# Local attention's mask: from a TensorE product to a VectorE addition in PSUM, with the score products of two heads written in turn

## The chip, the core and the metric

The kernel runs on one core of a Trainium2 chip. The metric is the device time of one execution in microseconds (us); the median of the runs counts.

## What is computed

A two-layer backbone over 256 context tokens and 256 latent tokens, width 1024. Each layer mixes tokens by three branches (a state space branch "S5", a latent attention "MLA", a windowed local attention), merges them by gates and an output projection, and then runs a mixture of 16 experts. The last layer updates the latent tokens alone. The part that matters here is the local attention of 8 query heads over 2 key heads, width 64:

```python
def window_branch(qc, kc, vc, ql, kl, vl, sink, row, col, update_ctx):
    ...
    valid = (jnp.abs(j - BLOCK - r) <= WINDOW) & (key_pos >= 0) & (key_pos < L)
    s_band = jnp.einsum('bnqkgd,bnskd->bnkgqs', qb, kb).astype(jnp.float32) * WIN_SCALE
    s_band = jnp.where(valid[None, :, None, None], s_band, NEG_INF)
    s_ctx = jnp.einsum('bnqkgd,bskd->bnkgqs', qpb, kc).astype(jnp.float32) * WIN_SCALE
    sk = jnp.broadcast_to(sink.astype(jnp.float32)[None, None, :, :, None, None], s_ctx.shape[:-1] + (1,))
    p = jax.nn.softmax(jnp.concatenate([s_band, s_ctx, sk], axis=-1), axis=-1)
    ...
    out_c = None
    if update_ctx:
        ...
        out_c = dense_attention(q_c, kc, vc, WIN_SCALE, sink).reshape(B, Lc, WIN_Q_HEADS * WIN_HEAD_DIM)
```

With 256 latent tokens and blocks of 128 there are two blocks of queries, and each sees the keys of both; the mask cuts one triangle of the block that is not its own.

## The kernel before

Everything is float32. A product that needs the full precision is made of three TensorE products of operands split into a high and a low part (`mm3`, line 411). A head is 64 wide, so the operands of one head lie on 64 partitions, rows 0 to 63 for the even head of a pair and rows 64 to 127 for the odd one.

`win_branch` (line 1237) runs once in each layer. It goes over 4 pairs of heads `hp` and 2 blocks of queries `qt`. For each it takes two PSUM tiles named `sc` (there are two such buffers in all, line 187), one for each head `a`, and fills each with 512 scores: three products for the context keys (columns 0 to 255), three for the latent keys (256 to 511), and one product of the identity with a constant mask of 128 x 128 that is accumulated onto 128 of these columns (line 1261). That product is in full float32 and appears as two records in the trace. `softmax` (line 1014) then reads the tile: VectorE takes the maximum of a row (`tensor_reduce`, line 1024), joins the sink (1025 to 1028), ScalarE takes the exponential (line 1031), VectorE sums, inverts and scales (1034 to 1037). After both blocks `attend` transposes the probabilities on TensorE into tiles `tp` and multiplies them with the values into `mm`. In the first layer (`full`) there are also two context tiles for each pair, with six products each and no mask.

TensorE's gaps are filled: `tick` issues work of other parts, in the first layer branch projections (tiles `F`) and products for the modulation parameters of later groups (tiles `ad`); in the second layer branch projections alone. The program goes through a scheduler that orders each engine's instructions ahead of the run; each engine then goes through its own list strictly in order. Weights come by DMAs that the SP queue issues.

After the local attention come the latent attention, the output projection and the layer norm, then the experts, whose 192 tiles of weights of 1 MB stream through a ring of buffers.

Of the kernel before, what the change touches and what calls it, by code (L numbers as in the profile page):

```python
# [31 lines left out]
# ---------------------------------------------------------------- shape-only constants  # L32
# [68 lines left out]
# ---------------------------------------------------------------- memory map of SBUF  # L101
class Arena:
    """column ranges of one SBUF tile; the range that has been free for longest is given first"""
# [31 lines left out]
    def alloc_at(self, name, at, want):  # L135
        """the columns at .. at + want, which are free"""
        assert name not in self.live and at % self.G == 0, name
        at, need = at // self.G, (want + self.G - 1) // self.G
        assert at + need <= self.n and None not in self.stamp[at:at + need], (name, self.live)
        return self.take(name, at, want)  # L140
# [17 lines left out]
class Net:  # L158
# [6 lines left out]
    # ------------------------------------------------------------ helpers  # L165
# [6 lines left out]
    def rot(self, name, cols, n, low=False, at=None):  # L172
        """n buffers used in turn: returns a function that gives the next one"""
# [21 lines left out]
    # ------------------------------------------------------------ work that fills the gaps of the tensor engine  # L195
# [3 lines left out]
    def tick(self, us):  # L199
        """issue about us of the work that waits in the queue"""  # L200
# [57 lines left out]
    def pow_(self, out, in_, e):  # L258
        """out = in_ ** e"""
# [7 lines left out]
    # ------------------------------------------------------------ layer norm statistics  # L267
    def ln_stats(self, x, mv, rstd):
        """x [128, 1024] -> mv [128, 2] mean/var, rstd [128, 1]"""
# [9 lines left out]
    def ln_apply(self, out, x, eng="v"):  # L279
        """out = (x - mean) * rstd"""  # L280
# [13 lines left out]
    def ln_affine(self, P, x, y, gb, again=True, eng="v"):  # L294
        """x = LN(P) g + b, P: halves of the columns; y: scratch; gives minus mean and 1 / deviation of x"""
# [34 lines left out]
    def ln_final(self, out, x, nm, r2):  # L330
        """out = (x + nm) r2"""
# [6 lines left out]
    # ------------------------------------------------------------ adaLN parameters  # L338
# [12 lines left out]
    def ada_group(self, l, g, bufs=None):  # L351
        """columns 2048 g .. of the adaLN parameters: mods 2g and 2g + 1"""
# [33 lines left out]
    def mod_row(self, l, m, s, dst, scale=1.0):  # L386
        """dst [128, 1024] = mod m of stream s on every partition"""
# [8 lines left out]
    # ------------------------------------------------------------ operands in two float32r parts  # L396
    def split(self, hi, lo, src, pool=True):
        """hi + lo = src exactly: 12 significant bits each"""
# [6 lines left out]
    def put(self, dst, src):  # L405
        """src into the parts dst [rows, 2, n]"""
# [8 lines left out]

    def block(self, tag, dtype):
        """a block that serves one purpose after another"""
# [3 lines left out]
    def branch_parts(self, l, b, oT, q0):  # L421
        """both parts of a branch output, [128, 4, 512 - q0]"""
# [17 lines left out]
    def wsplit(self, st, a, n, scale=None):  # L440
        """weights st [128, a, n] (times scale [128, a, n]) in two parts: a function of row k (and columns)"""
# [18 lines left out]
    def wchunk(self, src, a, n):  # L460
        """weights src [128, a, n] (a n <= 1024) in two parts"""
        return self.wsplit(self.wload(src, a, n), a, n)

    def modulated_split(self, l, x, in_place, step, stats):
        """both parts of modulate(LN(x))^T, 8 blocks of [128, 512] rows; step(h, kc) uses the rows 2 kc and 2 kc + 1"""
# [13 lines left out]
        # two blocks (row block, stream) at a time; of the second layer first those of the context  # L479
# [26 lines left out]
    # ------------------------------------------------------------ S5: matrices from the parameters  # L506
    def s5_setup(self, l, S, NP):
        """matrices of the layer from its parameters, NP group pairs at a time"""
# [72 lines left out]
        # powers a^1 .. a^4 (r: real, imaginary, minus real, minus imaginary)  # L581
# [16 lines left out]
        # phase of a^4 in turns, in [-1/2, 1/2]  # L598
# [19 lines left out]
        for j0 in range(0, 16, NP):  # L618
# [7 lines left out]
            # bb = q b  # L626
# [9 lines left out]
            # a^k bb and c a^k, state-major  # L636
# [25 lines left out]
            # chunk input matrices: (s, h) of a group on partitions, states on columns  # L662
# [1278 lines left out]
```

## Time and profile before

| what | us |
|---|---|
| three runs | 2166.41, 2170.84, 2172.0 |
| median | 2170.84 |
| span of the profiled execution | 2167.7 |

The profiled execution is a run of its own; the page gives its span, from the first to the last instruction, and nothing of what lies around that. The busy time of an engine in a stretch, and what ended an idle time, are read from stretches of the trace. A row of the timeline merges neighbouring instructions of one kind: its first column is the start, its second the time to the end of the last of them. Since products of TensorE are pipelined, what a group costs is read from its start to the start of the next row, not from its own duration.

### The profile page before, as it was taken

How to read it: one execution, taken by the hardware profiler on the slowest of the kernel's cores; microseconds unless marked ns; L12 is line 12 of the kernel's file. 1: busy time of each engine (PE TensorE's matmuls, PEld its weight loads, DVE VectorE, ACT ScalarE, POOL GpSimd, SP SyncE). 2: the span in 40 equal slices, each digit the busy share in tenths (PEclk: the TensorE clock that was granted, in tenths of full speed). 3: DMA queues.
4: the chain of work that ended last, by engine and by line, in shares of the span. 5: the costliest groups of instructions: out<-in, count | busy, mean ns of one | idle time of the engine just before them, and what ended most of it. 6: DMA issues, size and time to landing. Idle time of an engine off the chain costs nothing. (4 is left out here: it accounts for less than half of the span.)

```text
span 2167.7 us, 31197 instructions
## 1 busy us (share of the span) xinstructions
PE 1856.2 (86%) x12121; PEld 1117.8 (52%) x12121; DVE 1041.5 (48%) x2463; ACT 613.4 (28%) x1353; POOL 454.4 (21%) x592
## 2 busy tenths in 40 slices
PE   5998999999998799999798979889998766666665
PEld 2876666666776434343333358777786533222222
DVE  7767666644538512222555165978767311010102
ACT  2344343433434311010111054654553100000000
POOL 5735420000135100000434033642114000000000
PEclk8999999999999899999899989899999787686766
DMA  7234533265347799989899823242267799999996
GB/s 304 65 127 142 159 131 111 72 206 185 92 133 285 273 382 409 409 350 378 329 375 355 324 76 96 74 142 79 75 221 249 303 409 409 409 409 409 409 409 271
DMA packets 222163, 544.16 MB, mean 251 GB/s; under 512 B 18624, under 2 KB 101696, under 8 KB 221120
## 3 DMA queue, kind: packets, MB, share of 16 engines
q1 hardware_dynamic: 222016, 542.18, 67.6%
q8 instruction: 95, 1.56, 0.3%
q14 instruction: 52, 0.43, 0.1%
HBM read 541.09 MB, written 1.05 MB: 250 GB/s over the span
## 5 line engine op out<-in xcount | busy, mean ns | idle before, releaser
L243 PE MATMUL F<-h,wc 128*128 128x256 f32 (+1 forms) x1200 | 239.5, 351 | 13.9 <-ACT arena L1291 9.7
L400 ACT ACTIVATE wc<-arena 128x512 fp32r<-128x512 f32 (+2 forms) x280 | 170.2, 619 | 229.3 <-DMA arena<-in_w_in 49.4
L403 DVE TENSOR_TENSOR wc<-arena,wc 128x512 fp32r<-128x512 f32 (+2 forms) x205 | 163.8, 809 | 121.7 <-ACT wc L400 120.7
L243 PE MATMUL sc<-arena,xs 128*32 128x256 f32 (+1 forms) x1176 | 171.8, 535 | 56.7 <-DMA arena<-in_w_up 36.3
L243 PEld LDWEIGHTS F<-h,wc 128*128 128x128 f32 x1200 | 189.6, 197 | 47.9 <-ACT arena L1291 10.8
L246 PE MATMUL tp<-const,arena 128*128 128x128 f32 (+2 forms) x835 | 137.6, 291 | 62.8 <-DVE arena L1615 13.4
L403 POOL TENSOR_TENSOR wc<-arena,wc 128x512 fp32r<-128x512 f32 (+2 forms) x75 | 99.3, 1324 | 431.1 <-ACT wc L400 305.9
L243 PE MATMUL mm<-arena 128*32 128x256 f32 (+5 forms) x1076 | 168.1, 460 | 16.4 <-DMA arena<-in_w_down 8.0
L246 PEld LDWEIGHTS tp<-const,arena 128*128 128x128 f32 (+2 forms) x835 | 98.4, 146 | 120.8 <-issue 34.8
L1635 DVE TENSOR_TENSOR arena<-mm,arena 32x256 f32<-32x256 f32 (+1 forms) x96 | 48.9, 510 | 220.5 <-PE mm L243 208.7
L238 ACT ACTIVATE arena<-tp 128x512 f32<-128x512 f32 (+3 forms) x142 | 63.1, 474 | 311.9 <-PE tp L246 311.4
L260 POOL TENSOR_TENSOR lnq<-lnq,k 128x1 f32<-128x1 f32 x22 | 16.4, 747 | 574.5 <-DVE lnq L307 538.3
L243 PEld LDWEIGHTS sc<-arena,xs 128*32 128x32 f32 (+1 forms) x1176 | 54.4, 134 | 152.0 <-issue 81.9
L243 PE MATMUL sc<-h,xs 128*32 128x256 f32 (+1 forms) x760 | 118.7, 529 | 15.6 <-DMA h<-in_w_up 8.2
L1613 ACT ACTIVATE arena<-sc 128x512 f32<-128x512 f32 (+1 forms) x32 | 15.7, 490 | 366.3 <-PE sc L243 364.0
L243 PEld LDWEIGHTS mm<-arena 128*64 128x64 f32 (+2 forms) x1076 | 69.6, 137 | 91.5 <-issue 44.5
L243 PE MATMUL sc<-big,xs 128*32 128x256 f32 (+1 forms) x688 | 95.0, 522 | 15.5 <-DMA big<-in_w_gate 8.9
L1615 DVE TENSOR_TENSOR arena<-arena,sc 128x512 f32<-128x512 f32 (+1 forms) x32 | 17.7, 553 | 176.1 <-PE sc L243 175.7
L243 PE MATMUL mm<-wc,h 128*128 128x512 f32 (+2 forms) x288 | 78.4, 397 | 11.0 <-ACT h L492 6.1
L243 PE MATMUL F<-extra,wc 128*128 128x256 f32 (+1 forms) x432 | 85.0, 342 | 2.7 <-DVE arena L1326 2.4
L546 DVE TENSOR_TENSOR arena<-arena 128x64 f32<-128x64 f32 (+2 forms) x300 | 81.5, 318 | 10.7 <-POOL arena L549 4.7
L243 PEld LDWEIGHTS sc<-h,xs 128*32 128x32 f32 (+1 forms) x760 | 36.5, 132 | 86.8 <-issue 49.8
(345 smaller groups left out, 3246.6 us busy)
## 6 DMA issues: line engine op xcount, KB each, us to landing
arena<-in_w_gate SPq DMA_DIRECT2D x53, 1024.0 KB, 11.3
arena<-in_w_down SPq DMA_DIRECT2D x48, 1024.0 KB, 12.5
arena<-in_w_up SPq DMA_DIRECT2D x44, 1024.0 KB, 18.2
arena<-in_w_ada SPq DMA_DIRECT2D x82, 512.0 KB, 4.6
h<-in_w_down SPq DMA_DIRECT2D x41, 1024.0 KB, 10.3
h<-in_w_up SPq DMA_DIRECT2D x37, 1024.0 KB, 10.5
arena<-in_w_in SPq DMA_DIRECT2D x66, 512.0 KB, 3.8
big<-in_w_gate SPq DMA_DIRECT2D x30, 1024.0 KB, 15.1
```

Of the source, the lines that this page charges most:

```text
L238: self.nc.scalar.activation(out, in_, AF.Copy)
L243: return self.nc.tensor.matmul(out, lhsT, rhs, start=start, stop=stop, skip_group_check=True)
L246: self.nc.tensor.transpose(out, in_, self.c("idn")[:n, :n])
L260: self.nc.gpsimd.tensor_tensor(out, in_, e.to_broadcast(list(in_.shape)), op=OP.pow)
L400: nc.scalar.activation(hi, src, AF.Copy)
L403: eng.tensor_tensor(lo, src, hi.bitcast(F32), op=OP.subtract)
L546: tt = lambda o, a, b, op: v.tensor_tensor(o, a, b, op=op)
L1613: nc.scalar.activation(th, gu[0][:, :NF], AF.Tanh, scale=0.5)
L1615: v.tensor_tensor(th, th, gu[1][:, :NF], op=OP.mult)
L1635: v.tensor_tensor(YS[o:o + M, c * NF:(c + 1) * NF], yp[M * c:M * c + M, :NF], m5[M * c:M * c + M], op=OP.mult)
```

## The change

`mm3s` issues the three partial products of several outputs in turn. The score products of the two heads of a pair are written through it, for both blocks and for the context tiles. The mask product is gone; instead VectorE adds the mask to the 128 columns of the PSUM tile, in place. The rest of the diff removes comments.

```diff
+    def mm3s(self, outs, a, b, start, stop):
+
+        for i, j in ((0, 0), (0, 1), (1, 0)):
+            for out, a_, b_ in zip(outs, a, b):
+                self.mm(out, a_[i], b_[j], start and i + j == 0, stop and i == 1)
...
-                for a in range(2):
-                    self.mm3(sc[a][:, 0:256], two(QP[rows[a], hp], qc), two(KW[rows[a], kv], slice(0, 256)), True, True)
-                for a in range(2):
-                    self.mm3(sc[a][:, 256:512], two(QR[rows[a], hp], qs), two(KW[rows[a], kv], slice(256, 512)),
-                             True, False)
-                for a in range(2):
-                    self.mm(sc[a][:, off:off + 128], self.c("idn"), self.c(f"mask{qt}"), False, True)
+                own = range(2)
+                self.mm3s([sc[a][:, 0:256] for a in own], [two(QP[rows[a], hp], qc) for a in own],
+                          [two(KW[rows[a], kv], slice(0, 256)) for a in own], True, True)
+                self.mm3s([sc[a][:, 256:512] for a in own], [two(QR[rows[a], hp], qs) for a in own],
+                          [two(KW[rows[a], kv], slice(256, 512)) for a in own], True, True)
+                for a in own:
+                    far = sc[a][:, off:off + 128]
+                    self.nc.vector.tensor_tensor(far, far, self.c(f"mask{qt}"), op=OP.add)
...
-                    for a in range(2):
-                        self.mm3(sc[a][:, qt], two(QP[rows[a], hp], slice(qt * 128, qt * 128 + 128)),
-                                 two(KW[rows[a], kv], slice(0, 256)), True, True)
+                    self.mm3s([sc[a][:, qt] for a in range(2)],
+                              [two(QP[rows[a], hp], slice(qt * 128, qt * 128 + 128)) for a in range(2)],
+                              [two(KW[rows[a], kv], slice(0, 256)) for a in range(2)], True, True)
```

How the scheduler now orders the lists shows at three places. The number behind a tile's tag tells tiles apart: `sc134` is the odd head (rows 64 to 127) of the first pair's first block, `sc136` and `sc137` are its even and odd head in the second block, `sc140` its even context tile; `F` and `ad` are fill work. TensorE in the first layer, early in the local attention, before:

```order
L243 MATMUL sc134_2448<-big1117_2148,big0116_2147 128x256 x3
L243 MATMUL sc134_2448<-big1117_2148 128x256 x3
L243 MATMUL sc134_2448<-const_72 128x128
L243 MATMUL sc136_2510<-big1117_2148,big0116_2147 128x256 x3
L243 MATMUL sc136_2510<-big1117_2148 128x256 x3
L243 MATMUL sc136_2510<-const_72 128x128
L243 MATMUL ad152_2721<-arena_73,silu_c_64 32x512 x2
```

The same place after:

```order
L243 MATMUL sc134_2448<-big1117_2148,big0116_2147 128x256 x3
L243 MATMUL sc134_2448<-big1117_2148 128x256 x3
L243 MATMUL sc136_2510<-big1117_2148,big0116_2147 128x256 x3
L243 MATMUL sc136_2510<-big1117_2148 128x256 x3
L243 MATMUL ad152_2721<-arena_73,silu_c_64 32x512 x2
```

The mask products (`<-const`) are gone, and the products of an odd and an even head of neighbouring blocks now stand side by side; the six products of one tile still stand together, and the two heads of one block (`sc136`, `sc137`) are not in turn.

TensorE in the second layer, at the second to fourth tile of the local attention (`sc645` is the odd head of the first block, `sc647` and `sc648` the two of the second), before:

```order
L243 MATMUL sc645_10301<-big1628_10013 128x256 x3
L243 MATMUL sc645_10301<-const_72 128x128
L243 MATMUL sc647_10357<-big1628_10013,big0627_10012 128x256 x3
L243 MATMUL sc647_10357<-big1628_10013 128x256 x3
L243 MATMUL sc647_10357<-const_72 128x128
L243 MATMUL F649_10393<-extra0639_10227,wc_10337 128x256 x6
L243 MATMUL F649_10393<-extra0639_10227,wc_10340 128x256 x6
L246 MATMUL tp651_10408<-const_72,arena_73 128x128
L246 MATMUL tp652_10414<-const_72,arena_73 128x128
L243 MATMUL F657_10484<-extra0639_10227,wc_10478 128x256 x6
L243 MATMUL F657_10484<-extra0639_10227,wc_10481 128x256 x6
L243 MATMUL sc648_10358<-big1628_10013,big0627_10012 128x256 x3
```

and after:

```order
L243 MATMUL sc645_10301<-big1628_10013 128x256 x3
L243 MATMUL F649_10393<-extra0639_10227,wc_10337 128x256 x6
L243 MATMUL F649_10393<-extra0639_10227,wc_10340 128x256 x6
L243 MATMUL sc647_10357<-big1628_10013,big0627_10012 128x256 x3
L243 MATMUL sc647_10357<-big1628_10013 128x256 x3
L246 MATMUL tp651_10408<-const_72,arena_73 128x128
L246 MATMUL tp652_10414<-const_72,arena_73 128x128
L243 MATMUL sc648_10358<-big1628_10013,big0627_10012 128x256 x3
```

Here fill work moved between the tiles, which now come singly instead of in twos.

VectorE at the same place (`smst` holds the row statistics of a softmax), before:

```order
L1315 SCALAR_TENSOR_TENSOR arena_73<-arena_73,F646_10343 128x256
L1034 TENSOR_TENSOR smst_10316<-smst_10316 128x1
L1024 TENSOR_REDUCE smst_10326<-sc645_10301 128x1
L1035 RECIPROCAL smst_10316<-smst_10316 128x1
L1025 SCALAR_TENSOR_TENSOR smst_10326<-smst_10326,sink_10298 128x1
```

and after (line numbers from 1030 on are those of before plus 6):

```order
L1322 SCALAR_TENSOR_TENSOR arena_73<-arena_73,F646_10343 128x256
L1032 TENSOR_SCALAR smst_10316<-smst_10316 128x1
L1268 TENSOR_TENSOR sc645_10301<-sc645_10301,const_72 128x128
L1034 TENSOR_TENSOR smst_10316<-smst_10316,sink_10298 128x1
L1030 TENSOR_REDUCE smst_10326<-sc645_10301 128x1
L1040 TENSOR_TENSOR smst_10316<-smst_10316 128x1
L1031 SCALAR_TENSOR_TENSOR smst_10326<-smst_10326,sink_10298 128x1
```

The addition (line 1268) stands ahead of the maximum of its tile and is now the instruction that waits for TensorE.

## Rows read from the trace of the kernel before

**Rows 1.** The page: the span, and each engine's busy time.

```profile
span 2167.7 us, 31197 instructions
...
PE 1856.2 (86%) x12121; PEld 1117.8 (52%) x12121; DVE 1041.5 (48%) x2463; ACT 613.4 (28%) x1353; POOL 454.4 (21%) x592
```

**Rows 2.** Busy time by stretches (us from the span's start), one column an engine.

```profile
core 0: us, PE busy (x) PEld busy (x) DVE busy (x) ACT busy (x) POOL busy (x), PEclk, DMA share, GB/s
309.40:378.00 68.60, 68.60 (x369) 44.50 (x369) 43.26 (x139) 23.94 (x71) 5.01 (x4) 1.00 0.40 130
378.00:397.50 19.50, 17.49 (x109) 11.24 (x106) 13.94 (x56) 9.86 (x31) 0.00 (x0) 1.00 0.17 53
397.50:590.00 192.50, 191.07 (x992) 129.75 (x991) 103.09 (x243) 75.83 (x172) 19.42 (x16) 1.00 0.47 150
...
745.00:1190.00 445.00, 420.28 (x1976) 160.87 (x1978) 160.33 (x515) 57.01 (x147) 68.95 (x201) 0.98 0.95 367
1475.90:1507.90 32.00, 31.71 (x216) 27.02 (x215) 24.77 (x81) 13.46 (x39) 4.65 (x4) 0.95 0.21 66
1507.90:1523.20 15.30, 15.04 (x93) 10.53 (x91) 11.90 (x46) 7.73 (x23) 0.00 (x0) 1.00 0.11 36
...
1700.00:2167.70 467.70, 317.81 (x3279) 131.22 (x3278) 67.60 (x161) 26.26 (x63) 1.41 (x3) 0.76 0.98 389
```

**Rows 3.** Mask products of the two local attentions: count, duration min/median/max, first and last start.

```profile
L243 PE MATMUL sc<-const x32: 275/276/378, 310.3 to 392.8; 128*128 128x128 f32 x32
...
L243 PE MATMUL sc<-const x32: 275/377/580, 1476.9 to 1523.0; 128*128 128x128 f32 x32
```

**Rows 4.** TensorE's timeline in the first layer: start, duration, what; two masked tiles.

```profile
310.34 0.49 PE L243 MATMUL sc<-const 128*128 128x128 f32 x2
310.58 3.05 PE L243 MATMUL F<-extra,wc 128*128 128x512 f32 x12
...
315.45 0.49 PE L243 MATMUL sc<-const 128*128 128x128 f32 x2
315.87 0.62 PE L243 MATMUL sc<-big,big 64*128 64x256 f32 x3
```

**Rows 5.** The same timeline: a context tile alone, then two tiles of opposite row halves.

```profile
323.68 0.97 PE L243 MATMUL sc<-big,big 64*128 64x256 f32 x6
324.58 3.06 PE L243 MATMUL F<-extra,wc 128*128 128x512 f32 x12
...
328.22 0.98 PE L243 MATMUL sc<-big,big 64*128 64x256 f32 x9
...
329.47 0.49 PE L243 MATMUL sc<-const 128*128 128x128 f32 x2
```

**Rows 6.** VectorE's two-input groups by shape: count, busy us, mean ns, idle before.

```profile
L1542 DVE TENSOR_TENSOR arena<-arena,const 128x128 f32<-128x128 f32 x24 | 5.9, 288 | 4.5 <-PE F L243 3.1 <-PE ad L243 1.4
...
L1208 DVE TENSOR_TENSOR arena<-sc,const 128x256 f32<-128x256 f32 x10 | 4.1, 415 | 2.4 <-PE sc L243 2.4
```

**Rows 7.** Timeline, second layer: from the mask product to the row maximum.

```profile
1486.90 0.51 PE L243 MATMUL sc<-big 64*128 64x256 f32 x3
...
1487.34 0.49 PE L243 MATMUL sc<-const 128*128 128x128 f32 x2
...
1487.86 0.69 DVE L1024 TENSOR_REDUCE smst<-sc 128x1 f32<-128x512 f32 x1 [0.23 <-PE sc L243]
```

**Rows 8.** VectorE's timeline in the first layer: the row maximum of an unmasked tile.

```profile
356.90 0.69 DVE L1024 TENSOR_REDUCE smst<-sc 128x2 f32<-128x512 f32 x1 [0.51 <-PE sc L243]
```

**Rows 9.** TensorE's timeline: the products of that unmasked tile.

```profile
355.88 0.98 PE L243 MATMUL sc<-big,big 64*128 64x256 f32 x6
```

**Rows 10.** Timelines at the end of the second layer's local attention: exponential, then the buffer's next tile.

```profile
1518.16 0.69 ACT L1031 ACTIVATE arena<-sc,smst 128x512 f32<-128x512 f32 x1 [1.36 <-PE sc L243]
...
1518.99 0.62 PE L243 MATMUL sc<-big,big 64*128 64x256 f32 x3
```

**Rows 11.** First piece of the chain that ended last (start, us, what).

```profile
1678.29 0.06 DVE lnq L312
```

## Prediction, made before the changed kernel ran

> **What bounds the kernel now.** I read the page first: TensorE is busy for 86% of the span, VectorE for 48% [rows 1]. Such shares are means over stages, so the next view is the busy time by stretches [rows 2]. The local attention of the first layer runs from 309.4 to 397.5 us and falls in two. To 378.0 TensorE is busy in 68.60 of 68.60 us: fill work lies between the score tiles, and TensorE sets the pace. From 378.0 the fill work is used up and TensorE is busy in 17.49 of 19.50 us; it waits for the softmax now and then. The second layer's local attention (1475.9 to 1523.2 us) falls in two in the same way: to 1507.9 with fill work, TensorE 31.71 of 32.00 us but VectorE already 24.77; from there 15.3 us without. The stages behind pass a shift on. The latent attention of the first layer has TensorE at 191.07 of 192.50 us, and its experts have TensorE at 420 of 445 us while the DMA queues are 95% busy, but their loads are released by the mixers' end and move with it. The end of the kernel, from 1700 us on, is bound by DMA (98%, 389 GB/s) [rows 2]; what starts it is the layer norm at 1678 us, where the chain that ended last begins [rows 11]. So a microsecond saved in either local attention should be a microsecond at the end, and one lost likewise.
>
> **The change, part by part.**
>
> *The mask products go.* There are 32 records in each layer, two to a product: 16 products in each [rows 3]. What one costs TensorE is the time from its start to the next row's start: 0.24 us if a full-height product of tile F follows (310.34 to 310.58), 0.42 us if a 64-row product follows (315.45 to 315.87) [rows 4]; before a transpose it lies between these two. In the first layer's saturated stretch there are 12: five at 0.24 and seven at 0.42, that is 1.2 + 2.9 = 4.1 us. In the second layer's stretch to 1507.9 there are 10: three at about 0.25, three at about 0.32 and four at about 0.42, 3.4 us. The other 10 (four behind 378.0 at 1.6 us together, six behind 1507.9 at 2.4 us, waits included) lie where TensorE waits for the softmax.
>
> *The two heads in turn.* The order shows that this does not come about: the two PSUM tiles come free at different times, and the six products of a tile still stand in one piece in both layers. What comes about is a side effect: with no mask product between them, an odd head's tile and the even head's tile that follows stand next to each other. The trace has this twice already, behind the unmasked context tiles. One tile alone takes 0.90 us from its start to the next row (323.68 to 324.58); two neighbours in opposite row halves take 1.25 us (328.22 to 329.47) instead of 1.80 [rows 5]. So the halves partly run at once, and a new neighbourhood is worth 0.55 us. The order has five new full ones: three in the first layer's saturated stretch (1.65 us), one at that layer's end, one at the end of the second layer's. The Trainium skill, page "TensorEngine Tiling (Array Packing)", section "Tiling Modes", says that tiles of the array work independently and that a change of tiling mode drains the engine; the trace agrees on both, by the 1.25 us and by the 0.42 against 0.24 us. By that rule alone, with the issue in turn as the change words it, 20 pairs of tiles would each give such a saving, 11 us beyond the masks, against the 2.75 us of the five places that the order has.
>
> *VectorE adds 32 times.* No row shows a VectorE instruction that writes PSUM. The nearest rows: 288 ns for 128 x 128 from SBUF, 415 ns for 128 x 256 with one input in PSUM [rows 6]. I take the row of the same size, 0.29 us, 9.3 us for all; the bounds are 0.15 us (half of it, should neighbours overlap) and 0.42 us (the row of twice the columns).
>
> *The path of one tile.* On a masked tile the last scores end at 1487.41 (1486.90 and 0.51) and the maximum starts at 1487.86, 0.45 us later, with the mask product between them [rows 7]. On an unmasked tile the products end at 356.86 (355.88 and 0.98) and the maximum starts 0.04 us later [rows 8, 9]. The mask product thus put 0.41 us there; the addition puts 0.29 us and perhaps 0.03 us for a second step on VectorE. A tile's path is about 0.1 us shorter, not longer. The wait for TensorE is not new either: it moves from the maximum to the addition, with the same queue behind it (the sums, scalings and copies of the tile before).
>
> *What binds next.* In the first layer's saturated stretch VectorE needs 43.26 + 12 x 0.29 = 46.7 us of 62.9 us, so it can follow. There I count the whole 4.1 + 1.65 = 5.75 us. In the second layer's it needs 24.77 + 10 x 0.29 = 27.7 us, and TensorE would need 32.0 - 3.4 = 28.6 us. That leaves VectorE 0.9 us of idle time where it had 7.2 us, all in waits for others. The bounds are a gain of 3.4 us and a loss of 2.9 us; since the path of a tile gets no longer, I place it above the middle, at a gain of 1.7 us. In the two late stretches the softmax path sets the pace: at 1518.16 the exponential starts, lasts 0.69 us, and 0.14 us after its end the next tile of its buffer starts [rows 10]. I count nothing there; the bounds are 0 and 1.6 + 2.4 + 1.1 = 5.1 us. Other engines' lists keep their instructions, somewhat shifted against each other, into the first latent attention; SP moves a few weight loads against each other, while the DMA queues are 40% busy or less there [rows 2]. I give that no time.
>
> The sum is 5.75 + 1.7 = 7.45 us out of the span of 2167.7 us, 2160.25 us. The median of the runs stands 3.1 us above that span, and I carry this over: 2163.4 us.
>
> **The rivals.**
>
> *TensorE sets the pace throughout.* If VectorE follows in the second layer and the late stretches shorten too, the gain is all the masks, 4.1 + 3.4 + 1.6 + 2.4 = 11.5 us, and five neighbourhoods, 2.75 us: 14.3 us, 2156.6 us. For it: TensorE is above 89% busy in all four stretches. Against it: the 0.14 us in the late stretch.
>
> *The gain is taken by waits.* With less work between tiles, TensorE reaches the next tile earlier and waits until its buffer is free. If only the first layer's saturated masks hold and the second layer loses its 2.9 us, the gain is about 2 us: 2169 us. For it: VectorE's 27.7 of 28.6 us. Against it: in the first layer's saturated stretch TensorE had no wait at all, and 4.1 us less work is spread over 68.6 us.
>
> *VectorE becomes the bound: slower.* Every addition lies on VectorE's list ahead of sums and scalings that transposes wait for. If VectorE sets the pace in both layers, all 32 additions come on top and nothing that TensorE saves counts: 9.3 us more, 2180 us. It decides from the point where VectorE's work fills its stretch: in the second layer at 0.38 us an addition (24.77 + 10 x 0.38 = 28.6 us), just beyond my value; in the first not before 1.6 us. That the first layer would have to turn as well speaks against it.
>
> **How the numbers follow.** About 0.3%, 6.5 us, is what a measurement of this kernel can tell from no change. My forecast, 2163.4 us with 2159.5 to 2167 as its own range, has a chance of 0.55, and 0.7 of that lies below 2164.3 us. TensorE throughout (2156.6 us) has 0.16, the gain taken by waits (2169 us) 0.22, VectorE as the bound (2180 us) 0.07. So faster 0.55 x 0.7 + 0.16 = 0.545, rounded to 0.55, slower 0.07, and no change the rest, 0.38. The range takes in the first two and most of the third: 2156 to 2170.5 us.
>
> **What would show it.** The profile after should show no product from the mask constant in the local attentions, and 32 additions on 128 x 128 of about 0.29 us. TensorE's saturated stretch in the first layer should end 5 to 6 us sooner and still be above 98% busy. In the second layer the local attention should be 1 to 3 us shorter, with VectorE above 85% busy in its first part. The chain that ended last should begin some 7 us sooner. The forecast is wrong if an addition takes over 0.4 us, if TensorE shows new waits before score tiles or transposes in the first layer, or if the shift is there at 400 us and gone by 1700 us.

## The result and the profile after

The changed kernel takes 2181.47 us in the median of 4 runs (2176.81 to 2186.99), the kernel before 2170.28 us beside it: a ratio of 1.0057 (95% interval 1.0037 to 1.0076), 11 us slower. A later comparison with more runs gave 2180.75 against 2169.49 us, 1.0046 (1.0030 to 1.0061). The forecast was 2163.4 us with a range to 2170.5 us: its sign was wrong and the time lies outside the range.

The profiled execution is the slowest of the four. Its local attention of the first layer starts 2.8 us later than before (312.25 against 309.43 us), ahead of anything that the change touches; the later profile of the same kernel starts it at 309.46 us and ends 11 us behind the kernel before, so I use both. First the page of the profile after, the span and the engines' busy time, to be read beside [rows 1]:

```profile
span 2185.2 us, 31112 instructions
...
PE 1863.6 (85%) x12057; PEld 1118.6 (51%) x12057; DVE 1055.0 (48%) x2495; ACT 615.1 (28%) x1353; POOL 452.5 (21%) x592
```

TensorE has 64 records less (the mask products) and is busy 7.4 us longer. Work was taken away, and what is left takes longer. The group of the additions, from the view by line (count, busy us, mean ns, idle time before and its releaser), and one addition in VectorE's timeline with the maximum behind it:

```profile
L1268 DVE TENSOR_TENSOR sc<-sc,const 128x128 f32<-128x128 f32 x32 | 9.5, 296 | 10.2 <-PE sc L243 10.1
```

```profile
1517.53 0.29 DVE L1268 TENSOR_TENSOR sc<-sc,const 128x128 f32<-128x128 f32 x1
1517.86 0.69 DVE L1030 TENSOR_REDUCE smst<-sc 128x1 f32<-128x512 f32 x1
```

The 32 additions are there, 0.30 us each, and the maximum starts 0.33 us behind the addition's start. These were the sizes that the prediction took. Now the busy time by stretches, after; the first line is the filled part of the first layer's local attention, the next three stretches were cut at the granted clock's changes:

```profile
core 0: us, PE busy (x) PEld busy (x) DVE busy (x) ACT busy (x) POOL busy (x), PEclk, DMA share, GB/s
312.20:378.00 65.80, 64.46 (x341) 40.19 (x340) 45.51 (x148) 23.63 (x71) 4.75 (x4) 1.00 0.41 135
...
381.10:394.60 13.50, 12.67 (x48) 7.24 (x48) 7.97 (x32) 5.54 (x21) 0.00 (x0) 0.50 0.13 41
401.60:408.30 6.70, 5.25 (x21) 3.46 (x20) 5.81 (x27) 2.65 (x12) 0.00 (x0) 0.50 0.02 3
...
1531.40:1541.50 10.10, 9.57 (x38) 6.41 (x37) 6.80 (x29) 4.04 (x12) 0.00 (x0) 0.50 0.01 2
```

The column to read is PEclk. Before, it stood at 1.00 in all of the first layer's local attention [rows 2]. After, it falls to 0.50, the lower of the two levels (1.2 instead of 2.4 GHz), for 13.7 and 6.8 us in the first layer, and for 6.8 and 10.2 us in the second layer beyond the 3.4 us that the kernel before also has at that stage's begin. TensorE's timeline around the falls (start, duration, what, and in brackets the wait and what ended it):

```profile
378.19 0.87 PE L246 MATMUL tp<-const,arena 128*128 128x128 f32 x6 [1.03 <-DVE arena L1043]
379.43 0.33 PE L246 MATMUL tp<-const,arena 128*128 128x128 f32 x1 [0.36 <-ACT arena L238]
...
381.68 1.92 PE L243 MATMUL ad<-arena,silu_c 128*32 128x512 f32 x4 [1.35 <-DMA arena<-in_w_ada]
...
400.85 2.32 PE L243 MATMUL sc<-big,big 64*128 64x256 f32 x12 [1.76 <-ACT arena L1037]
404.47 2.80 PE L246 MATMUL tp<-const,arena 128*128 128x128 f32 x10 [1.31 <-DVE arena L1043]
```

Within 5 us TensorE waits three times, 2.74 us together: for a scaling of the softmax (1.03 us), for a copy (0.36 us), and for a load of adaLN weights (1.35 us). By the record of the granted clock the fall comes at 381.05 us, so only the first two waits lie ahead of it; the third lies around it, and in the second profile just behind it (fall at 377.15 us, wait from 377.31 us). From there every product takes about twice its time: four adaLN records 1.92 us, where the same four take 1.05 us in the kernel before. Behind 394.7 us the clock is back; a wait of 1.76 us follows, the clock falls again at 401.53 us, and a wait of 1.31 us lies in that second piece. The kernel before also waits at this place, 0.36, 0.84, 0.41 and 0.36 us between 378.4 and 385.2 us, and its clock doesn't fall. Its last products of F and its wait for the adaLN load:

```profile
371.36 2.80 PE L243 MATMUL F<-extra,wc 128*128 128x512 f32 x11
...
380.82 1.05 PE L243 MATMUL ad<-arena,silu_c 128*32 128x512 f32 x4 [0.84 <-DMA arena<-in_w_ada]
```

The chain that ended last begins with the same instruction as in [rows 11], 17.85 us later:

```profile
1696.14 0.06 DVE lnq L312
```

**A balance of TensorE's time.** From the first score product of the first layer's local attention to the last score product of its latent attention, each product is given the time from its start to the next product's start, less the wait between. Where the granted clock is 0.5, half of that goes to a line of its own and the rest to the kind of product. The columns are the kernel before, the changed one (second profile) and three experiments told below, and each ends two or three transposes (0.2 to 0.3 us) behind that last product; us:

| kind | before | after | three pairs | held early | first held |
|---|---|---|---|---|---|
| score products | 39.80 | 37.66 | 38.10 | 38.23 | 37.35 |
| mask products | 5.78 | 0 | 1.49 | 0 | 0 |
| adaLN products (`ad`) | 35.79 | 38.92 | 36.70 | 37.73 | 36.76 |
| tiles F | 99.18 | 99.27 | 99.01 | 99.18 | 99.07 |
| transposes and tiles mm | 90.20 | 90.65 | 90.83 | 90.27 | 91.16 |
| waits | 3.44 | 7.51 | 4.03 | 4.02 | 5.11 |
| lost to clock 0.5 | 0 | 8.72 | 6.14 | 3.34 | 0 |
| sum | 274.19 | 282.71 | 276.31 | 272.78 | 269.45 |

The savings are all there: 5.78 us of masks and 2.14 us of score products side by side. Against them stand 4.1 us of new waits, 3.1 us of adaLN products and 8.7 us of half clock. The first profile of the changed kernel gives the same: waits 7.78, adaLN 39.33, clock 9.07 us. The sum of the waits alone doesn't tell what the clock takes: with three pairs 4.03 us of waits go with 6.14 us lost to it, first held waits 5.11 us and loses nothing. (The Trainium skill, page "TensorE: Matmul & The Clock Gate", section "Terms", prices a reduced clock at the time spent there times the part that is missing; for 20.5 us at half clock that would be 10.2 us, an estimate. The balance has less, since 3 us of the 20.5 were waits.)

The adaLN line has a cause of its own. Two rows of the changed kernel from the latent attention:

```profile
434.40 1.04 PE L243 MATMUL ad<-arena,silu_c 128*32 128x512 f32 x2
...
460.10 1.06 PE L243 MATMUL ad<-arena,silu_c 128*32 128x512 f32 x8
```

One product of 32 columns (two records) costs as much as four that stand side by side (eight records). The new order scatters these products, 26 rows of them in this stage instead of 22 with the same 140 records, although nothing of the change lies in that stage. That is 2.2 of the 3.1 us; the rest comes from one row more in the local attention itself.

In the second layer the same count, over local and latent attention, is 144.44 us before and 150.33 and 147.78 us in the two profiles after: masks 5.4 and side-by-side scores 0.6 us less, waits 3.5 to 3.9 us more, clock 0.5 for 6.3 to 8.3 us more.

### The profile page after: what moved, and what is told of

It reads as the page before. It is cut to its first block, busy times and chain, and to the rows that moved or that the text cites. A ratio compares the mean times of both kernels' runs of the same rounds, so it can differ in the third digit from the quotient of the medians.

```text
span 2185.2 us, 31112 instructions
## 1 busy us (share of the span) xinstructions
PE 1863.6 (85%) x12057; PEld 1118.6 (51%) x12057; DVE 1055.0 (48%) x2495; ACT 615.1 (28%) x1353; POOL 452.5 (21%) x592
## 3 DMA queue, kind: packets, MB, share of 16 engines
HBM read 541.09 MB, written 1.05 MB: 248 GB/s over the span
## 5 line engine op out<-in xcount | busy, mean ns | idle before, releaser
L246 PE MATMUL tp<-const,arena 128*128 128x128 f32 (+2 forms) x835 | 142.8, 299 | 67.5 <-DVE arena L1622 13.5
L243 PE MATMUL mm<-arena 128*32 128x256 f32 (+5 forms) x1076 | 174.2, 472 | 19.4 <-DMA arena<-in_w_down 10.4
L1621 DVE SCALAR_TENSOR_TENSOR arena<-arena,sc 128x512 f32<-128x512 f32 (+1 forms) x32 | 17.7, 554 | 134.1 <-ACT arena L1620 134.0
```

The lines of the kernel that those rows point to most:

```text
L243: return self.nc.tensor.matmul(out, lhsT, rhs, start=start, stop=stop, skip_group_check=True)
L246: self.nc.tensor.transpose(out, in_, self.c("idn")[:n, :n])
L1621: v.scalar_tensor_tensor(th, th, 1.0, gu[0][:, :NF], op0=OP.add, op1=OP.mult)
```

## The experiments

The theories: **A**, TensorE is left without work behind the score tiles at the end of the local attention, waits, and then runs at clock 0.5. **B**, VectorE's additions are the cost by themselves. **C**, the scheduler's new order of other work is the cost. **D**, no effect of the change, but a chance of the run. The two heads in turn have no run of their own, but the two runs below with the addition in one layer alone write the score products in the old order. From the first score product of that layer's local attention to the last of its latent attention, their traces have the same instructions in the same order as the changed kernel's first profile, in the first layer, and its second, in the second layer (1395 and 939 products on TensorE, and the lists of VectorE, ScalarE and GpSimd), as far as names and shapes tell tiles apart. So issuing the two heads in turn changes nothing there; the change is the mask alone.

**No mask at all.** The changed kernel without

```
-                for a in own:
-                    far = sc[a][:, off:off + 128]
-                    self.nc.vector.tensor_tensor(far, far, self.c(f"mask{qt}"), op=OP.add)
```

> The changed kernel without the 32 additions: the mask is left out of the local attention altogether. The changed kernel stands 11 us above the one before. Theory A (TensorE has less to do in the late stretches, waits there, and its granted clock falls to 0.5, as it did at 381.0 to 394.7 and 401.5 to 408.4 us of the changed kernel's trace): TensorE's work is that of the changed kernel, so rows at clock 0.5 stay in the local attention and the time stays above the kernel before, 2172 to 2181 us. Theory B (the additions are the cost, 0.33 us on the path of each tile, 32 of them 10.6 us): the time falls by that much, to 2170 us, or below it by up to the 7.5 us of the masks saved on TensorE.

Measured: 2172.35 us, ratio 1.0005 (0.9991 to 1.0019). A kernel that does neither the products nor the additions is no faster than the one before. The time is just inside A's bounds (2172 to 2181 us) and 2.4 us above the 2170 us that B gave. The rows tell more: in the first layer's local attention the clock stands at 0.5 in two pieces.

```profile
373.90:384.00 10.10, 8.62 (x32) 4.72 (x34) 4.61 (x19) 2.78 (x11) 0.00 (x0) 0.50 0.19 62
394.40:404.50 10.10, 9.12 (x29) 6.84 (x30) 6.24 (x32) 4.34 (x16) 0.00 (x0) 0.50 0.01 2
```

So half clock comes without an addition. But 9 us do go with the additions; B isn't done with.

**Both.** The changed kernel with the mask product put back ahead of the addition:

```
+                for a in range(2):
+                    self.mm(sc[a][:, off:off + 128], self.c("idn"), self.c(f"mask{qt}"), False, True)
```

> The changed kernel with the mask product put back beside the addition (the mask is applied twice). VectorE's additions stay, TensorE's work is that of the kernel before. Theory A (the clock): no row at clock 0.5 inside the first layer's local attention, and the time comes back to 2170 us plus 0.33 us for each tile of the late stretches, 10 of them, 2173 us. Theory B (the additions): the path of a tile gets longer by the product as well, 0.24 to 0.42 us for each of 32, and the time is 2181 us or more, up to 2192 us.

Measured: 2183.12 us, 1.0057 (1.0037 to 1.0077), as B expected and against A. Half clock in the first layer went down to 10.2 us but not away: the addition on top of the product makes a tile's path longer, and waits of 1.95 us (the adaLN load) and 1.09 us are still there. More work for TensorE on the path of the tiles is no cover.

**Part of the first layer.** The kernel before with the addition where `add` holds, the product elsewhere:

```
+                add = full and hp < 3
...
+                    if add:
+                        self.nc.vector.tensor_tensor(far, far, self.c(f"mask{qt}"), op=OP.add)
```

> The kernel before with the addition in place of the product only in the first layer, for the first three pairs of heads (12 of 32 tiles): those lie in the stretch that is filled with other work for TensorE. Theory A: TensorE has work behind every tile there, no wait and no row at clock 0.5, and the late stretch is that of the kernel before; the gain of the 12 products stays, 4 us and up to 1.65 us for neighbouring tiles, 2165 us. Theory B: 12 additions of 0.33 us cost 4 us against 4 us saved, 2170 us; if nothing of the saving counts, 2174 us.

Measured: 2171.38 us, 1.0010 (0.9996 to 1.0024). My expectation from A (2165 us, no half clock) was wrong; the 2170 us of B are within the noise of the time, but B has no half clock in it. By the balance the products' 4.3 us and 1.7 us of score products are saved and 6.1 us lost to the clock. TensorE's timeline:

```profile
374.35 0.88 PE L246 MATMUL tp<-const,arena 128*128 128x128 f32 x6 [1.03 <-DVE arena L1037]
...
377.86 1.92 PE L243 MATMUL ad<-arena,silu_c 128*32 128x512 f32 x4 [1.37 <-DMA arena<-in_w_ada]
...
380.12 1.65 PE L243 MATMUL sc<-big,big 64*128 64x256 f32 x9
```

The last pair of heads has the very instructions of the kernel before, yet its score products run at half speed: nine records take 1.65 us, 0.97 us in the kernel before. The saved time let TensorE finish the fill work sooner; it then met the softmax and the adaLN load, which did not come sooner by as much, and paid for it with 13.7 us at clock 0.5. Saved time upstream had become waits downstream.

**The whole first layer** (`add = full`), **and the second alone** (`add = not full`):

> The kernel before with the addition in place of the product in the whole first layer, and the second layer as before. Of the 17 us between the two profiled runs some 12 arose in and behind the first layer's local attention (375 to 480 us) and 5 in the second's. Theory A: rows at clock 0.5 in the late stretch of the first layer's local attention as in the changed kernel, none new in the second layer's; about two thirds of the 11 us, 2177 to 2178 us, so the last pair of heads (against the kernel with three pairs) costs some 12 us. Theory B: half of the additions, half of the loss, 2175 us, and the last pair costs a quarter of it, 1.5 us. If the loss of the second layer is larger than the trace says, 2174 us or less.

> The kernel before with the addition in place of the product in the second layer alone. First layer alone stood 8 us above the kernel before, the whole change 11 us; if the layers add, 2173 to 2174 us, with the rows at clock 0.5 of the changed kernel in the second layer's local attention (17 us beyond those of before). If the second layer alone costs nothing (below 2171 us), the 5 us that the two profiled runs showed there come from something that the first layer's change brings along.

Measured: 2177.47 us, 1.0039 (1.0025 to 1.0053) for the first layer, 2169.85 us, 1.0005 (0.9993 to 1.0016) for the second. So 8.5 of the 10 to 12 us come from the first layer, with the clock's fall (20.5 us) and the scattered adaLN products (38.92 us) of the changed kernel; the second alone costs 1 us, and can't be told from nothing; the 2173 to 2174 us of layers that add up did not come. The last pair of the first layer costs 0.29%, 6 us; both theories had it wrong (12 and 1.5 us).

**Fill work held back.** The test of A: the last two of the eight fill blocks of the first layer (F, products of the S5 branch) wait for an output of the local attention, by a small product that reads it and is overwritten at once. VectorE's work stays as it is.

```
+            after = self.HOLD.get((l, b, 2 * d2 + i))
+            if after is not None:
+                self.mm(pp[:, 256:320], self.c("idn"), self.held[:, after, 256:320], True, True)
             for k in range(4):
                 self.mm3(pp[:, q0:], w(k, ds), (oh[:, k], ol[:, k]), k == 0, k == 3)
...
+        self.held = oT
...
+    HOLD = {(0, 0, 6): 1, (0, 0, 7): 2}
```

> The changed kernel, with the last two of the eight fill blocks of the first layer (tile F, 12 products each) held back until the outputs of the second and of the third pair of heads are there: a 64-column product of that output, overwritten at once, stands ahead of each. They then lie in the late stretch, between the score tiles of the last pairs, where the changed kernel's TensorE waits; VectorE's list of work is the same. The order of the first latent attention also comes back to eight adaLN products in a row, as in the kernel before (the changed kernel has them scattered; 102 of them took 13.45 us before and 16.47 us there). Theory A with C (waits that end at clock 0.5, and scattered adaLN products): no row at clock 0.5 in the first layer's local attention, the 8 us that this layer costs (first layer alone: 2177.5 us) are gone and the 3 us that the first three pairs saved stay: 2168 to 2172 us. Theory B (the path over VectorE): nothing changes there, 2181 us.

Measured: 2167.64 us, 0.9991 (0.9981 to 1.0000): 12 to 14 us of the changed kernel's time are gone, though two small products (0.24 us each, from start to the next start) were added. From the first score product to the last of the latent attention it takes 270.59 us, half clock costs 1.7 instead of 8.7 us, and the adaLN products 36.75 instead of 38.92 us. B expected 2181 us. Not all of it is cover in the late stretch: between the two profiles (the changed kernel's second and this one) 12.1 us are won in the stages of the balance and 4.0 us in the stages from there to the second layer, where the scheduler's order differs too, and 6.4 us are lost again in the second layer. A's "no row at clock 0.5" came nearly: 3.4 us are left, and none in a second profile.

**The control**: the same two lines in the kernel before.

> The control: the kernel before, mask products and all, with the same two fill blocks of the first layer held back. Its late stretch has waits of 2 us and no row at clock 0.5. Theory A: little to win, 2168 to 2171 us. If holding back is a gain by itself, whatever masks the scores, it falls by as much as the changed kernel does, to 2160 us.

Measured: 2169.09 us, 0.9998 (0.9988 to 1.0008). Where TensorE had its cover, holding work back brings nothing.

**Held in both layers**, with `(1, 0, 6): 1, (1, 0, 7): 2` beside the two entries:

> The same with the last two fill blocks of the second layer held back as well. Theory A: rows at clock 0.5 go from the second layer's local attention too (20.5 us of it in the changed kernel, 3.4 us before), 4 us less than the kernel with the first layer held, and up to 3.4 us of mask products saved: 2161 to 2167 us. Theory B: VectorE was already the fuller engine in this stretch, so that moved fill work changes nothing: the same as the kernel with the first layer held, within 2 us.

Measured: 2168.73 us, 0.9994 (0.9982 to 1.0006), nothing beyond the first layer's hold. In the second layer A's expectation failed: 1.5 us of waits went from its local attention, but 20.5 us of half clock stood at the stage's begin, as in the kernel held in the first layer alone (below).

**Held early**: both blocks wait for the second pair only (`(0, 0, 6): 1, (0, 0, 7): 1`), so that the last pair is bare again while the order of the latent attention is that of the kernel before.

> The changed kernel, both fill blocks held back only until the second pair's outputs: they run in the third pair, and the late stretch is as bare as in the changed kernel, but the order of the first latent attention behind it is word for word that of the kernel before (adaLN products in rows of eight). It tells the clock from the order. Theory A, the clock alone: rows at clock 0.5 stay in the late stretch, and of the 8 us of the first layer only the 3 us of the scattered adaLN products go: 2177 to 2179 us. Theory C, the order alone: the loss of the first layer goes nearly all, 2170 to 2173 us.

Measured: 2170.46 us, 1.0000 (0.9986 to 1.0013), the value of C. But the profile doesn't give it to C alone: of the 9.9 us by which its column in the balance is shorter than that of the changed kernel, 5.4 are clock, 3.5 waits and 1.2 adaLN products. The wait for the adaLN load is gone, since its product stands elsewhere, one wait of 1.89 us is left, and 6.8 us at clock 0.5 follow it. So it didn't separate the two as I had meant; it shows that the place of two blocks decides over 10 us.

**The changed kernel again, and three more variants in the same comparison.**

> The changed kernel once more, unaltered, so that it stands beside the three below in the same comparison: 2181 us by its first runs (2176.8 to 2187.0). Its profile is a second sample of the clock's fall: by theory A again 10 us or more at clock 0.5 within the first layer's local attention, and more in the second's; if the first profile was a chance, none.

Measured: 2180.75 us, 1.0046. The falls of the clock in the first layer last 13.7 and 6.8 us again and stand between the same rows, as also with the first layer alone. That speaks against D.

**The version that beats both**: the addition in the first layer alone, with its two fill blocks held.

> The addition in the first layer alone (2177.5 us without more), with the two fill blocks held back as before. Theory A: the first layer's loss goes and its saved products stay, and the second layer is that of the kernel before: 2163 to 2167 us, faster than the kernel before. Theory B: 16 additions stay, 2175 us or more. If the shortening by 3.6 us that the kernel with both layers showed at the end of the first latent attention is given back later at the begin of the second layer's local attention, as in that kernel, 2169 us.

Measured: 2164.53 us, 0.9969 (0.9958 to 0.9980), 6.7 us faster than the kernel before and 16 us faster than the changed one, as A expected and not B. By stretches:

```profile
core 0: us, PE busy (x) PEld busy (x) DVE busy (x) ACT busy (x) POOL busy (x), PEclk, DMA share, GB/s
309.70:378.00 68.30, 67.25 (x373) 42.57 (x374) 48.95 (x175) 25.86 (x85) 2.01 (x2) 1.00 0.41 130
378.00:394.50 16.50, 14.04 (x81) 9.30 (x78) 12.24 (x47) 7.91 (x23) 2.55 (x2) 1.00 0.06 13
1468.00:1481.50 13.50, 13.41 (x56) 11.89 (x56) 6.09 (x22) 4.04 (x12) 2.00 (x2) 0.50 0.11 40
```

The clock stays at 1.00 through the first layer's local attention, which ends 3 us sooner. TensorE is busy for only 14.04 of 16.50 us at the end: it still waits, in pieces of 0.2 to 0.7 us, with fill blocks between, and no fall follows them in this profile (a second one, below, has 3.4 us at clock 0.5 here).

**No mask, held**: the kernel without products and additions, with the hold. It measures the additions where the cover holds.

> The kernel without the 32 additions and without the mask products (the mask is left out), with the two fill blocks of the first layer held back. It bounds what the additions themselves cost where the cover holds: the same kernel with the additions has 2167.6 us. Theory A: they are covered in the first layer, some 2 us in the late stretches, 2164 to 2168 us. Theory B: 32 times 0.33 us less, 2157 us.

Measured: 2162.36 us, 0.9956 (0.9940 to 0.9972), between the two expectations. Together with the others this gives a small table of ratios, each to the kernel before in its own comparison:

| mask by | fill as scheduled | two blocks held |
|---|---|---|
| product | 1 | 0.9998 |
| addition | 1.0046 | 0.9991 |
| neither | 1.0005 | 0.9956 |

Taking the products away is worth 0.42% (9 us) with the cover and nothing without it. Putting the additions in costs 0.35 to 0.41% (7.6 to 8.9 us), 0.24 to 0.28 us each, with the cover or without (0.52% without it by the first comparison's 1.0057). So the times give the additions a price of the size that B named. That it is paid where the additions stand, as B says, isn't shown. Without the cover, the second profile of the changed kernel and that of no mask differ by 3.6 us in the first layer's balance, and not by waits (7.51 against 8.06 us) but by score products (1.9 us) and adaLN products (1.9 us) that stand side by side less often; by -0.5 us in the second layer; and by 3.8 us in the stages between, which no edit touches. With the cover it is 4.0 us in the first layer (1.7 of half clock, 1.0 each of waits and adaLN products, 0.6 of score products), 7.2 us in the second, where half clock costs 18.3 against 9.9 us, and -3.4 us between. In the balance, then, most of that price is order and clock again. By the same balance, A and C are why nothing came in for the products.

**Second profiles.** At the begin of the second layer's local attention TensorE waits 1.2 to 1.3 and 2.0 us for a copy in every kernel, and the clock then falls: for 3.4 us in the kernel before, the changed one and seven others, for 13.7 or 20.5 us in four with held blocks. Two of these, first held and the kernel before with the hold (13.7 us each), have the same TensorE instructions there as the kernel before.

> The kernel before, a second profile. In its first one TensorE's clock did not fall in the first layer's local attention, and at the begin of the second layer's it stood at 0.5 for 3.4 us. If such a fall belongs to the order of the work and its waits, both come again (0 us, 3.4 us); if it is a chance of the execution, 10 us or more may show at either place.

> The addition in the first layer alone with the held fill blocks, a second profile. Its first had no clock 0.5 in the first layer's local attention and 13.7 us of it at the begin of the second layer's, where the kernel before had 3.4 us with the same instructions and the same waits ahead (1.3 and 2.0 us). If the length belongs to the kernel, 13.7 us again; if to the execution, another value, 3.4 or 20.5 us, and the span is shorter or longer by about half the difference, 5 us.

> The changed kernel with the held fill blocks, a second profile. Its first had 20.5 us at clock 0.5 at the begin of the second layer's local attention and 13.7 us more behind 1514 us. If that belongs to the kernel, 34 us again and a span of 2168 us; if to the execution, less, and the span is shorter by half of what is missing, down to some 2160 us.

Measured, one run each: before 3.4 us again, and no half clock in the first layer; first held 3.4 us instead of 13.7; held 20.5 and 13.7 us, exactly as in its first profile, but none in the first layer's local attention, where its first profile had 3.4 us. The first held kernel, second profile, where the first had 0.50 from 1468.0 to 1481.5:

```profile
1471.70:1475.00 3.30, 3.30 (x16) 3.08 (x16) 1.87 (x7) 0.74 (x2) 0.72 (x1) 0.50 0.46 164
1475.10:1518.70 43.60, 43.04 (x293) 34.15 (x293) 34.36 (x120) 20.50 (x60) 3.93 (x3) 1.00 0.16 49
```

So the length of such a fall isn't a property of the instructions alone. The spans of the two executions differ by 0.6 us only, since the second lost elsewhere what it won here (3.4 us at clock 0.5 in the first layer, later starts). What sets the length stays open, and with it a few us of the second layer's share in any one profile.

## Why the prediction was wrong, point by point

- **Masks removed** (4.1 + 1.6 us in the first layer, 3.4 + 2.4 in the second): right. The balance has 5.78 and 5.4 us.
- **Neighbours of opposite halves** (five places of 0.55 us, 2.75 us): right, 2.14 and 0.6 us. That the heads are not issued in turn was right too, and stronger than said: with the old order of the products the lists of the two layers come out the same.
- **The addition's duration and a tile's path** (0.29 us; 0.1 us shorter): right by the rows (0.30 us, 0.33 us to the maximum).
- **The additions are covered in the first layer's saturated stretch** (cost nothing): wrong by some 2 to 3 us. VectorE had room (45.51 of 65.8 us), but with no mask at all and the hold, the first layer's column is 4.0 us shorter than with 16 additions and the hold (266.58 against 270.59 us). Of that, 1.7 us are half clock, which the second profile of the kernel with the additions doesn't have; the rest is fewer waits, more score products side by side, and adaLN products less split. Room on the engine was the wrong question: with the additions the order is another. That they shift when tiles come ready is the likely reason, not a measured one.
- **The late stretches count nothing, bounds 0 and a gain of 5.1 us**: this is the step that failed. It let the lower bound end at nothing because the softmax set the pace there. In the kernel before the last products of F end at 374.1 us; in the second profile after they end at 370.6 us (first row below), so TensorE comes 3.5 us sooner to what follows them. The adaLN load that it then waits for lets it go on only 2.2 us sooner (378.66 instead of 380.82 us), and the softmax makes it wait 1.03 us where it hadn't to. The 4.1 us of new waits could have been bounded: they are little more than these 3.5 us. That much of the stretch then runs at half clock, 8.7 us more, no row of before showed in that stage. A row nearby did (second row below, from the kernel before): at the second layer's begin it waits 1.99 us and runs at 0.50 behind it for 3.4 us. I had read that stretch's clock of 0.95 [rows 2] and made nothing of it.

```profile
369.00 1.64 PE L243 MATMUL F<-extra,wc 128*128 128x512 f32 x6
...
1475.30 0.70 PE L243 MATMUL sc<-arena,const 128*128 128x256 f32 x2 [1.99 <-ACT arena L238]
```

- **Other lists, into the first latent attention: "I give that no time"**: wrong by 2.2 us in the latent attention and 0.9 us ahead of it, by the adaLN products. The duration of a lone product was in the trace before.
- **Second layer, a gain of 1.7 us, bounds +3.4 and -2.9**: alone it measured a loss of 1 us (a gain of 1.5 to a loss of 3.5), within the bounds but for the end of that interval. The way there was another than VectorE's filling: in that run's profile 5.4 us of masks are saved, and 3.8 us go to waits and 4.8 us to half clock beyond the kernel before.
- **The rival "The gain is taken by waits" (2169 us, 0.22)** came nearest in its mechanism: new waits took the gain, 4.1 us in the first layer and 3.5 to 3.9 us in the second. It missed the first layer, the clock and the order. Its sum was off besides: the first layer's 4.1 us less the second's 2.9 us are 1.2 us, not 2.
- **The rival "VectorE becomes the bound" (2180 us, 0.07)** came nearest in time, and its price for the additions (9.3 us) is nearly what the times give them. Its mechanism didn't come: VectorE is busy in 45.51 of 65.8 us in the first layer's filled part, and in the second layer, where it was to decide, the change alone costs 1 us. The loss lies in the first layer, which it had spoken against.
- **What would show it**: I had named new waits ahead of score tiles or transposes in the first layer as a sign of failure; they are the signature of what happened. The forecast of 5.75 us for the first layer came nearest in the kernel that keeps TensorE covered: first held is 6.7 us faster in all, and its first layer's stages are 4.7 us shorter in the one profile and 3.4 us in the other.

What stays open: the shares of clock and order in the first layer's 8.5 us are read from the balance, not from an experiment that changes one and keeps the other, since each edit let the scheduler write a new order. And that a wait brings the clock's fall is suggested by where the falls stand, and by the held kernels, in which the longer waits and most of the half clock go together; no run here moved the clock alone, and why the kernel before waits at the same place without a fall stays open. So does what the hold changed in the stages behind.

## What to carry to other kernels

Work taken off the engine that sets the pace was a gain here only where something else to do stood behind it: ask of each saved microsecond which load or softmax it will now wait for, and price the stretch behind that wait at half clock as well. Where a scheduler writes the order, removing instructions also reorders work that wasn't touched; compare the lists as far as they differ, and cost each place where products that ran side by side are split. If the change then disappoints, moving fill work into the new gap (two blocks here, 12 to 14 us) is tried before the change is dropped.

## What the runs showed of the hardware that I had not expected

- Waits of 1.03 and 0.36 us on TensorE within 3 us stood ahead of 13.7 us at clock 0.5, in four executions of three kernels (changed, first layer alone, three pairs), although TensorE was busy in 12.67 of 13.50 us of it. Waits of 0.2 to 0.7 us with fill blocks between them (first held and held, 2.46 us of waits in 16.50 us in the one) were followed by none in two executions and by 3.4 us in two others.
- Behind the same waits and with the same instructions the lower clock lasted 3.4 us in one execution of first held and 13.7 us in another; another kernel gave 20.5 us twice. The Trainium skill, page "TensorE: Matmul & The Clock Gate", section "Part 1: The HAM clock gate (the "warmup" mystery)", says that the point at which the clock rises varies from run to run, by some 500 ns to either side. These rows agree that it varies, but by 10 us.
- A lone product of 32 columns (two records, 1.04 us) costs as much as four side by side (eight records, 1.06 us).
- VectorE adds 128 x 128 from PSUM to PSUM in 0.30 us, within 0.02 us of the same shape in SBUF [rows 6].
